# Order of the high and low products in a split-weight GEMM of a two-layer hybrid encoder

## The chip, the cores and the metric

The kernel runs on one core of a Trainium2 chip. The metric is the device time of one execution in microseconds (us): 2810.59 us is the median of three runs of the kernel before the change.

## What is computed

Two layers of a bidirectional encoder for one sequence of 256 tokens and 2048 channels, all in 32-bit floats:

```
u = RMSNorm(h);  z = u W_in                # 51 blocks of 128 columns
h += concat[A(z_A), B(z_B), C(z_C), D(z_D)] W_out
h += relu(RMSNorm(h) W_up)^2 W_down        # 2048 -> 8192 -> 2048
h += (p[i] W_ple) * sigmoid(RMSNorm(h) W_gate)
```

A is differential attention, B a gated linear recurrence (HGRN2), C a set of centred mean pools, D bidirectional RWKV-7 time mixing. Each works on 512 of the 2048 channels.

## The kernel before

Tokens are the free dimension (256 columns), channels lie on the partitions in chunks of 128. Every large product is a sum over chunks k of the contraction (16 for a contraction of 2048) of a 128x128 block of weights by a 128x256 piece of activations, into one PSUM tile of 128 output channels. Weights and activations are each kept as a high and a low part (of the type fp32r), and a product leaves out low by low.

**Weights.** `wsplit` (L132 to L144) loads 1024 weight columns (eight chunks k) with one DMA on SP, then for each 512 columns (a *part*, four chunks) ScalarE copies the high part `wh` (L140) and VectorE subtracts it from the raw weights for the low part `wl` (L142). `wh` and `wl` have two buffers each in the mixers and four in the pool `wide` behind them; the raw weights have four.

**Activations.** `split` stores each chunk as [hi | lo], 512 columns.

**Products.** For one chunk k, `mm2` (L154) issues two: `wh` by [hi | lo], 512 columns (L158), and then `wl` by hi, 256 columns (L159), which gives two half sums that `add_to` (L161) or its like adds later. `mm3` (L146) issues three of 256 columns (L150 to L152) into one half. Both products of a chunk come before those of the next chunk. `gemm_block` (L165) makes one block of 128 output channels: two loads of eight chunks each. It gets its PSUM tile from `K.accum`: pool `pg` with two buffers in the mixers and in the first half of the output projection, four (`pgw`) from then on.

**Stages of a layer.** The mixers call `z` (L225) for each block of `w_in`: 15 blocks for D with `mm3`, 36 for A, B and C with `mm2`. D works on four pairs of heads: `first` (L498), which needs neither an inverse nor the state, then `invert`, then `second` (L665) on the pairs 1, 3, 0, 2 with small products named psW, psX, psZ, pss, psst, psr, psy, psm and psv. Its result goes to DRAM through `put` (L414). What `first` leaves for `second` lies in a store `sp`; that of pair 0 is the tile `sp0`, which has the tag "h" and so the place of the residual h (L498). B's head makes its attention matrix in seven levels, each with a product psbl (L1015), a masked copy (L1017) and two multiplications (L1022, L1023) on VectorE and a rearranging copy (L1011) on ScalarE.

The output projection follows (L277 to L316), by `out_block`. Its contraction is cut in two: 12 chunks of mixer outputs that are done early (`mh1`, `w_out1`, with `mm2`) and 4 that are done last (`mh2`, `w_out2`, with `mm3`). Its h is loaded afresh from DRAM (L286 to L289) into the place with the tag "h". From block m = 9 on (L293) the weights come from the pool `wide`, which takes the room that the mixers held. The MLP (up and down in four quarters) and the gate with the per-layer embedding are `gemm_block` with `mm2`.

**Order.** The program text gives only the order in which the work is handed over. A scheduler then sets the order on each engine, by its own model of how long everything takes; so D's and B's small products stand among the products of `w_in` and of the output projection. DMAs are issued in the order in which they stand on SP.

Of the kernel before, what the change touches and what calls it, by code (L numbers as in the profile page):

```python
# [8 lines left out]
F32 = mybir.dt.float32  # L9
# [7 lines left out]
P = 128  # L17
# [35 lines left out]
# the output projection's contraction in the order in which the heads' outputs come  # L53
# [18 lines left out]
def trunk(ctx: ExitStack, tc: tile.TileContext, xT, pT, w_in, w_out1, w_out2, w_up, w_down, w_gate, w_ple, pvec,  # L72
# [10 lines left out]
    # every function used (Copy, Identity, Square, Exp, Ln) is in this one table set  # L83
    A.preload_act_table_set("natural_log_exp_and_others")

# [31 lines left out]
    # derived parameter columns  # L117
# [4 lines left out]
    # 0..14 token-shift own weight, 15..18 1-ka, 19 subln gain, 20..23 lb, 24..27 1-lb, 28 -lambda, 29..32 lb-1  # L122
# [9 lines left out]
    def wsplit(src, cols=1024):  # L132
        """Load weights and split them exactly into two float32r parts, in halves of 512 columns."""
# [12 lines left out]
    def mm3(ps, parts, b, act, start, stop):  # L146
        wh, wl = parts[b // 4]
        b %= 4
        w1, w2 = wh[:, b * P:(b + 1) * P], wl[:, b * P:(b + 1) * P]
        T.matmul(ps[:, :S], w1, act[:, :S], start=start, stop=False)  # L150
        T.matmul(ps[:, :S], w1, act[:, S:], start=False, stop=False)  # L151
        T.matmul(ps[:, :S], w2, act[:, :S], start=False, stop=stop)  # L152

    def mm2(ps, parts, b, act, start, stop):  # L154
        """The same with a weight part's loads shared: ps holds two halves, whose sum is the result."""
        wh, wl = parts[b // 4]
        b %= 4
        T.matmul(ps, wh[:, b * P:(b + 1) * P], act, start=start, stop=False)  # L158
        T.matmul(ps[:, :S], wl[:, b * P:(b + 1) * P], act[:, :S], start=False, stop=stop)  # L159
# [5 lines left out]
    def gemm_block(wsrc, m, act, mm=mm2, nk=KC, before=None):  # L165
        """One block of 128 output channels over nk chunks of the contraction."""
        ps = K.accum("acc")
        for u in range(nk // 8):
            w = wsplit(wsrc[m, u])
            for j in range(8):  # L170
                k = u * 8 + j
                if before is not None:
                    before(k)
                mm(ps, w, j, act[:, k], k == 0, k == nk - 1)
        return ps

    def split(dst, src, scale=None):
        """dst = [hi | lo] of src (times a per-channel scale)."""
# [7 lines left out]
    def rsqrt(dst, src, eps, scale=1.0):  # L186
        """dst = (src * scale + eps) ** -0.5"""
        A.activation(dst, src, AF.Ln, bias=eps, scale=scale)
        A.activation(dst, dst, AF.Exp, scale=-0.5)

    def sigmoid(dst, src, scale=None, bias=None):
        """dst = 1 / (1 + exp(-(src)))  ; bias is added to src (given already negated)."""
# [32 lines left out]
    def z(m, dst):  # L225
        """dst = a block of w_in's outputs. (D's, which come first, leave less of the vector engine's time.)"""
# [13 lines left out]
    def front():  # L240
        """Room for the next layer's input. It goes into w_in without RMSNorm's token scales, which come later."""
# [7 lines left out]
    def enter(c):  # L249
        """The first layer's input, a chunk of channels at a time."""  # L250
# [9 lines left out]
    for l in range(DEPTH):  # L260
# [7 lines left out]
        # in two parts: the second for the heads that are done last  # L268
# [8 lines left out]
        def out_block(wsrc, mh, n, mm):  # L277
            ps = K.accum("acc")
            for o in range(0, n, 8):
                nn = min(8, n - o)  # L280
                w = wsplit(wsrc[:, o * P:(o + nn) * P], nn * P)
                for j in range(nn):
                    k = o + j
                    mm(ps, w, j, mh[:, k], k == 0, k == n - 1)
# [7 lines left out]
        for m in range(KC):  # L292
            if m == 9:  # L293
                # outside the mixers there is room to load weights far ahead
# [19 lines left out]
        def norm():  # L314
            """The token scales of RMSNorm, applied to the products behind it."""
# [55 lines left out]
        for mm in range(4):  # L371
            pw = wsplit(w_ple[l, mm])
            for b in range(4):
                m = mm * 4 + b
                pp = pe.tile([P, 512], F32, tag="acc2", name="acc2", bufs=2)
                for k in range(2):
                    mm3(pp, pw, b * 2 + k, ph[:, k], k == 0, k == 1)
# [58 lines left out]
# w_in blocks in device order: D's wl, al, gl; D's k, r, v for the four pairs of heads; then four rounds of a C group,  # L436
# A's q, k, v (a head) and B's q, f, b, i, g (a head)
# What the first half of D's work on a pair of heads leaves to the second, in columns, for each direction.
# Instances are (head, chunk of 128 tokens); matrices are [s, t].
# [4 lines left out]
class MixerD:  # L444
    def __init__(self, K):
# [16 lines left out]
        # tanh(x) = 2 / (1 + exp(-2x)) - 1  # L462
# [27 lines left out]
    def slot(self, c):  # L490
        """A pair's place: the residual's or that of the MLP's input, which nothing else needs now."""
# [6 lines left out]
    def first(self, c, base):  # L498
        """All of a pair of heads that needs neither the inverse nor the state."""
# [10 lines left out]
        # normalised key direction  # L510
# [10 lines left out]
        # token-major v  # L521
# [12 lines left out]
        for d in range(2):  # L534
# [11 lines left out]
            # cumulative decay within chunks of 128, one pad column  # L546
# [23 lines left out]
            # [kk | r] with the decay up to t, [-b | k] with the inverse decay up to s  # L570
# [605 lines left out]
```

## Time and profile before

| what | value |
|---|---|
| median of 3 runs | 2810.59 us |
| lowest and highest run | 2810.06 and 2812.09 us |
| span of the profiled execution | 2811.6 us |
| instructions | 47293 |
| VectorE busy | 1986.4 us, 71% of the span |
| ScalarE busy | 1631.4 us, 58% |
| weights `wh` on ScalarE (L140) | 1704 times, mean 631 ns |
| weights `wl` on VectorE (L142) | 1704 times, mean 692 ns |
| bytes read from HBM | 471.51 MB |

No time was recorded for the profiled execution other than its span, which runs from the first recorded instruction to the last.

In the rows below PE is TensorE's multiplication, PEld its weight load (which overlaps PE), DVE VectorE, ACT ScalarE, SP the queue that issues DMAs. L158 is line 158 of the kernel. A duration of a matmul includes its passage through the array, so that two which follow each other overlap in the list: the distance between starts is the pace. The granted clock (PEclk) is a share of full speed.

### The profile page before, as it was taken

The numbers are of one execution on the slowest core, as the hardware profiler recorded it, in microseconds if no ns is written. First come the engines' busy times: TensorE is split into PE (matmuls) and PEld (weight loads), VectorE is DVE, ScalarE is ACT, GpSimd is POOL, SyncE is SP. The second block draws the span as 40 slices with busy tenths as digits, with TensorE's granted clock in tenths as the row PEclk, the third lists the DMA queues.
The fourth block names the chain that finished last, engine by engine and source line by source line (L and its number), as shares of the span: only waits on it lengthen the run. The fifth ranks groups of instructions, "written<-read, shape, count | busy, mean of one in ns | idle before, by whom it ended". The sixth has DMA issues, their size and how long they took to land.

```text
span 2811.6 us, 47293 instructions
## 1 busy us (share of the span) xinstructions
PE 2773.0 (99%) x16934; PEld 2378.5 (85%) x16934; DVE 1986.4 (71%) x4139; ACT 1631.4 (58%) x3342; POOL 57.5 (2%) x98
## 2 busy tenths in 40 slices
PE   8999999999999999999999999999999999999999
PEld 7877788898888888888898777888888888888888
DVE  7678877786666666667767697677766666666776
ACT  6555656476645546456765665565665465564565
POOL 0000110000000000000000001100000000000000
PEclk9999999999999999999999999999999999999999
DMA  6444445565555555555545444545655555555564
GB/s 211 151 138 142 157 125 194 198 198 187 187 187 187 187 185 185 186 187 197 173 161 161 128 150 148 167 145 177 199 187 188 187 187 184 188 185 187 187 198 158
DMA packets 186211, 494.40 MB, mean 176 GB/s; under 512 B 43732, under 2 KB 66900, under 8 KB 185848
## 3 DMA queue, kind: packets, MB, share of 16 engines
q1 hardware_dynamic: 185976, 491.39, 53.2%
q8 instruction: 133, 2.18, 0.3%
q14 instruction: 102, 0.84, 0.1%
HBM read 471.51 MB, written 19.80 MB: 175 GB/s over the span
## 4 chain that ended last, share of the span: by engine, by line
PE 92%; DVE 3%; ACT 2%; DMA 2%; issue 1%; POOL 0%; SPq 0%; DVEq 0%; POOLq 0%; ACTq 0%
PE acc L158 49%; PE acc L159 25%; PE acc L152 3%; PE acc L150 2%; PE acc L151 2%; PE psam L591 2%; DVE wl L142 1%; PE psbl L1015 1%; PE psrv L600 1%; PE pss L749 1%; PE psl L925 1%; ACT wh L140 1%; DMA raw<-in_w_out 1%; DMA ot<-o_scr 0%; PE psy L772 0%
## 5 line engine op out<-in xcount | busy, mean ns | idle before, releaser
L140 ACT ACTIVATE wh<-raw 128x512 fp32r<-128x512 f32 x1704 | 1073.7, 631 | 1023.1 <-PE acc L158 859.3
L142 DVE TENSOR_TENSOR wl<-raw,wh 128x512 fp32r<-128x512 f32 x1704 | 1177.1, 692 | 642.5 <-ACT wh L140 631.0
L158 PE MATMUL acc<-u,wh 128*128 128x512 f32 x3200 | 1154.0, 401 | 1.1 <-ACT wh L140 1.1
L159 PE MATMUL acc<-u,wl 128*128 128x256 f32 x3200 | 918.7, 288 | 7.8 <-DVE wl L142 7.4
L158 PEld LDWEIGHTS acc<-u,wh 128*128 128x128 f32 x3200 | 603.5, 189 | 146.2 <-ACT wh L140 5.7
L158 PE MATMUL acc<-act,wh 128*128 128x512 f32 x2048 | 723.9, 399 | 0.0
L159 PEld LDWEIGHTS acc<-u,wl 128*128 128x128 f32 x3200 | 606.1, 189 | 29.2 <-DVE wl L142 16.8
L159 PE MATMUL acc<-act,wl 128*128 128x256 f32 x2048 | 575.2, 281 | 0.0
L158 PEld LDWEIGHTS acc<-act,wh 128*128 128x128 f32 x2048 | 384.8, 188 | 96.2
L159 PEld LDWEIGHTS acc<-act,wl 128*128 128x128 f32 x2048 | 386.9, 189 | 0.0
L158 PE MATMUL acc<-ug,wh 128*128 128x512 f32 x512 | 181.6, 397 | 0.0
L150 PE MATMUL acc<-u,wh 128*128 128x256 f32 x480 | 137.9, 287 | 11.4 <-ACT u L183 9.8
L152 PE MATMUL acc<-u,wl 128*128 128x256 f32 x480 | 141.9, 296 | 2.2 <-DVE wl L142 2.0
L159 PE MATMUL acc<-ug,wl 128*128 128x256 f32 x512 | 143.4, 281 | 0.0
L158 PE MATMUL acc<-mh,wh 128*128 128x512 f32 x384 | 138.0, 398 | 0.7 <-ACT wh L140 0.6
L151 PE MATMUL acc<-u,wh 128*128 128x256 f32 x480 | 137.3, 286 | 0.7 <-DVE u L184 0.6
L158 PEld LDWEIGHTS acc<-ug,wh 128*128 128x128 f32 x512 | 96.0, 188 | 21.1
L159 PE MATMUL acc<-mh,wl 128*128 128x256 f32 x384 | 110.8, 289 | 0.9 <-DVE wl L142 0.9
L150 PEld LDWEIGHTS acc<-u,wh 128*128 128x128 f32 x480 | 91.8, 191 | 15.7 <-ACT u L183 10.0
L152 PEld LDWEIGHTS acc<-u,wl 128*128 128x128 f32 x480 | 91.6, 191 | 12.6 <-DVE wl L142 6.4
L159 PEld LDWEIGHTS acc<-ug,wl 128*128 128x128 f32 x512 | 96.7, 189 | 0.7
L151 PEld LDWEIGHTS acc<-u,wh 128*128 128x128 f32 x480 | 91.5, 191 | 2.5 <-DVE u L184 1.7
(320 smaller groups left out, 2808.4 us busy)
## 6 DMA issues: line engine op xcount, KB each, us to landing
raw<-in_w_up SPq DMA_DIRECT2D x256, 512.0 KB
raw<-in_w_down SPq DMA_DIRECT2D x256, 512.0 KB
raw<-in_w_in SPq DMA_DIRECT2D x204, 512.0 KB
raw<-in_w_gate SPq DMA_DIRECT2D x64, 512.0 KB
raw<-in_w_out SPq DMA_DIRECT2D x32, 512.0 KB
raw<-in_w_out SPq DMA_DIRECT2D x64, 256.0 KB
h<-in_xT SPq DMA_DIRECT2D x8, 512.0 KB
m_scr<-sp SPq DMA_DIRECT2D x16, 256.0 KB
```

The source lines that it names most:

```text
L140: A.activation(wh[:, :n], raw[:, o:o + n], AF.Copy)
L142: V.tensor_tensor(wl[:, :n], raw[:, o:o + n], wh[:, :n].bitcast(F32), ALU.subtract)
L150: T.matmul(ps[:, :S], w1, act[:, :S], start=start, stop=False)
L151: T.matmul(ps[:, :S], w1, act[:, S:], start=False, stop=False)
L152: T.matmul(ps[:, :S], w2, act[:, :S], start=False, stop=stop)
L158: T.matmul(ps, wh[:, b * P:(b + 1) * P], act, start=start, stop=False)
L159: T.matmul(ps[:, :S], wl[:, b * P:(b + 1) * P], act[:, :S], start=False, stop=stop)
L591: T.matmul(ps[:, x * S:(x + 1) * S], BK[hs, j, x, :], KR[j][hs].rearrange("p a b -> p (a b)"), start=True, stop=True)
L600: T.matmul(pv_[hs, S + j * P:S + (j + 1) * P], vt[:, j, hs], AV[:, 1, :], start=False, stop=True, skip_group_check=True)
L749: T.matmul(ps[:, d * P + h * 64:d * P + (h + 1) * 64], Zs[d][:, h * 2 + j, :], rk(d, j)[:, h] if st == 0 else RH[:, d, h, :], start=True, ...
L925: T.matmul(pl[:, :S], qn[ms, qs], kn[ms, :], start=True, stop=True)
L1015: T.matmul(p2[:, i * P:(i + 1) * P], kc[:, i * P:(i + 1) * P], strided(Q, i * P, [[2 * hh, P // (2 * hh)], [W + hh, 2], [1, hh]]), start=T ...
```

## The change

`mm2` and `mm3` no longer take one chunk but one part of the weights and a group of its chunks, four of them (two for `w_ple`): all products with the high part come first, then all with the low part. The callers pass groups: `gemm_block`, `out_block` and the product with `w_ple`. `before(k)`, with which a caller splits an input chunk just ahead of its product, is called for the four chunks of a group ahead of the group. No instruction is added or removed; the sums are added up in another order. (In the changed kernel these functions stand a few lines further down: L161 and L163 are what L158 and L159 were.)

```diff
-    def mm3(ps, parts, b, act, start, stop):
-        wh, wl = parts[b // 4]
-        b %= 4
-        w1, w2 = wh[:, b * P:(b + 1) * P], wl[:, b * P:(b + 1) * P]
-        T.matmul(ps[:, :S], w1, act[:, :S], start=start, stop=False)
-        T.matmul(ps[:, :S], w1, act[:, S:], start=False, stop=False)
-        T.matmul(ps[:, :S], w2, act[:, :S], start=False, stop=stop)
...
+    def mm3(ps, part, group):
+        wh, wl = part
+        for b, act, start, stop in group:
+            w1 = wh[:, b * P:(b + 1) * P]
+            T.matmul(ps[:, :S], w1, act[:, :S], start=start, stop=False)
+            T.matmul(ps[:, :S], w1, act[:, S:], start=False, stop=False)
+        for b, act, start, stop in group:
+            T.matmul(ps[:, :S], wl[:, b * P:(b + 1) * P], act[:, :S], start=False, stop=stop)
...
-        T.matmul(ps, wh[:, b * P:(b + 1) * P], act, start=start, stop=False)
-        T.matmul(ps[:, :S], wl[:, b * P:(b + 1) * P], act[:, :S], start=False, stop=stop)
+        for b, act, start, stop in group:
+            T.matmul(ps, wh[:, b * P:(b + 1) * P], act, start=start, stop=False)
+        for b, act, start, stop in group:
+            T.matmul(ps[:, :S], wl[:, b * P:(b + 1) * P], act[:, :S], start=False, stop=stop)
...
-            for j in range(8):
-                k = u * 8 + j
+            for o in range(0, 8, 4):
+                ks = range(u * 8 + o, u * 8 + o + 4)
                 if before is not None:
-                    before(k)
-                mm(ps, w, j, act[:, k], k == 0, k == nk - 1)
+                    for k in ks:
+                        before(k)
+                mm(ps, w[o // 4], [(k % 4, act[:, k], k == 0, k == nk - 1) for k in ks])
...
-                for j in range(nn):
-                    k = o + j
-                    mm(ps, w, j, mh[:, k], k == 0, k == n - 1)
+                for i in range(0, nn, 4):
+                    ks = range(o + i, o + i + 4)
+                    mm(ps, w[i // 4], [(k % 4, mh[:, k], k == 0, k == n - 1) for k in ks])
```

Since the scheduler works out its order anew, the small products move too. Three places follow. All are of TensorE in the first layer's output projection; `acc<-mh` are the products of a block (`wh` the high, `wl` the low part), the others belong to the mixers, and a final number as in x4 counts equal rows.

First, the second block of the projection. Before the change:

```order
L158 MATMUL acc<-mh_5837,wh 128x512
L719 MATMUL psX<-U_2734,sp_1115 64x64 x4
L1015 MATMUL psbl<-bQ,bkc 128x128 x2
L159 MATMUL acc<-mh_5837,wl 128x256
L158 MATMUL acc<-mh_5837,wh 128x512
L159 MATMUL acc<-mh_5837,wl 128x256
```

With the change:

```order
L161 MATMUL acc<-mh_5837,wh 128x512 x4
L951 MATMUL psan<-t_5425,cst 128x256
L992 MATMUL psbv<-cst,z 128x128 x2
L163 MATMUL acc<-mh_5837,wl 128x256 x4
L161 MATMUL acc<-mh_5837,wh 128x512 x4
L723 MATMUL psX<-U_2571,sp_2565 64x64 x4
L163 MATMUL acc<-mh_5837,wl 128x256 x4
```

Where high and low products took turns, four high ones now precede four low ones, and small products stand between the two fours.

Second, the stretch behind the second block. Before the change small products stand singly among those of the blocks:

```order
L159 MATMUL acc<-mh_5837,wl 128x256
L1015 MATMUL psbl<-bQ,bkc 128x128 x2
L158 MATMUL acc<-mh_5837,wh 128x512
L749 MATMUL pss<-sp_1115,Tm 128x64 x2
L159 MATMUL acc<-mh_5837,wl 128x256
```

With the change, from the last product of the second block on (66 small products stand before the third block; the first of them):

```order
L163 MATMUL acc<-mh_5837,wl 128x256 x4
L1006 MATMUL psbd<-x_5434,bkc 128x128 x2
L1019 MATMUL psbl<-bQ,bkc 128x128 x2
L729 MATMUL psZ<-Tm,W 64x64 x4
L753 MATMUL pss<-sp_2565,Tm 128x64 x2
L1019 MATMUL psbl<-bQ,bkc 128x128 x2
L753 MATMUL pss<-sp_2565,Tm 128x64 x2
L1019 MATMUL psbl<-bQ,bkc 128x128 x2
L760 MATMUL psst<-SA,sp_2565 64x64 x4
L1019 MATMUL psbl<-bQ,bkc 128x128 x2
L744 MATMUL psr<-S_2673,sp_2565 128x128 x2
L1019 MATMUL psbl<-bQ,bkc 128x128 x2
```

The third block's products have moved behind all of these; `sp_2565` is the store of pair 0, in the place of h.

Third, the end of D's last `second`, ahead of block m = 9. Before the change:

```order
L159 MATMUL acc<-mh_5837,wl 128x256
L785 MATMUL psm<-t_2878,cst 128x256
L158 MATMUL acc<-mh_5837,wh 128x512
...
L790 MATMUL psv<-t_2884,cst 128x256
L159 MATMUL acc<-mh_5837,wl 128x256
```

With the change; the last row but one is the first of block m = 9:

```order
L163 MATMUL acc<-mh_5837,wl 128x256 x4
L776 MATMUL psy<-sp_1115,SA 64x128 x2
L781 MATMUL psy<-sp_1115,S_2836 128x128
L776 MATMUL psy<-sp_1115,SA 64x128 x2
L781 MATMUL psy<-sp_1115,S_2836 128x128
L789 MATMUL psm<-t_2878,cst 128x256
L794 MATMUL psv<-t_2884,cst 128x256
L161 MATMUL acc<-mh_5837,wh 128x512 x4
L163 MATMUL acc<-mh_5837,wl 128x256 x4
```

The products of a block that stood between psy, psm and psv now stand ahead of all three.

## Rows read from the trace of the kernel before

**Rows 1.** The page: busy time and the chain that ended last, shares of the span.

```profile
PE 2773.0 (99%) x16934; PEld 2378.5 (85%) x16934; DVE 1986.4 (71%) x4139; ACT 1631.4 (58%) x3342; POOL 57.5 (2%) x98
...
PE 92%; DVE 3%; ACT 2%; DMA 2%; issue 1%; POOL 0%; SPq 0%; DVEq 0%; POOLq 0%; ACTq 0%
```

**Rows 2.** L158 in a stretch of the MLP: us; PE, PEld busy (count); PEclk; DMA share; GB/s.

```profile
800.00:900.00 100.00, 100.00 (x284) 53.18 (x283) 1.00 0.56 188
```

**Rows 3.** Who waited until a weight part was made: all low parts; L158 (us, times).

```profile
  DVE wl L142: 35.9, 70
...
  ACT wh L140: 8.9, 22
```

**Rows 4.** Timeline in the mixers: start, us, engine, line, operation [idle before <- releaser].

```profile
250.83 0.42 DVE L1023 TENSOR_TENSOR bK<-bK,bF 128x256 f32<-128x256 f32 x1
...
251.00 0.39 PE L158 MATMUL acc<-u,wh 128*128 128x512 f32 x1
...
251.50 0.68 DVE L142 TENSOR_TENSOR wl<-raw,wh 128x512 fp32r<-128x512 f32 x1
...
252.24 0.39 PE L159 MATMUL acc<-u,wl 128*128 128x256 f32 x1 [0.85 <-DVE wl L142]
```

**Rows 5.** Groups by line and form: count | busy us, mean ns | idle before.

```profile
L159 PE MATMUL acc<-u,wl 128*128 128x256 f32 x3200 | 918.7, 288 | 7.8 <-DVE wl L142 7.4
...
L159 PE MATMUL acc<-act,wl 128*128 128x256 f32 x2048 | 575.2, 281 | 0.0
...
L152 PE MATMUL acc<-u,wl 128*128 128x256 f32 x480 | 141.9, 296 | 2.2 <-DVE wl L142 2.0
```

**Rows 6.** Windows (PE, PEld, DVE, ACT, POOL; PEclk; DMA; GB/s) and a timeline row.

```profile
348.00:351.00 3.00, 1.34 (x20) 1.07 (x20) 1.44 (x4) 2.00 (x7) 0.53 (x1) 1.00 1.02 419
351.00:355.00 4.00, 4.00 (x20) 3.49 (x19) 2.54 (x5) 1.59 (x4) 0.00 (x0) 0.52 0.59 168
...
1740.40:1747.20 6.80, 6.80 (x29) 6.01 (x27) 4.08 (x8) 2.31 (x6) 0.00 (x0) 0.50 0.52 158
...
350.79 0.38 PE L725 MATMUL psZ<-Tm,W 64*64 64x64 f32 x3 [1.28 <-ACT W L722]
```

**Rows 7.** Timeline of TensorE in the MLP.

```profile
589.68 0.62 PE L158 MATMUL acc<-u,wh 128*128 128x512 f32 x2
590.13 0.28 PE L159 MATMUL acc<-u,wl 128*128 128x256 f32 x1
590.25 0.40 PE L158 MATMUL acc<-u,wh 128*128 128x512 f32 x1
590.49 0.28 PE L159 MATMUL acc<-u,wl 128*128 128x256 f32 x1
```

**Rows 8.** Timeline rows ahead of block m = 9.

```profile
516.50 0.44 PE L772 MATMUL psy<-sp,SA 128*64 128x128 f32 x4
...
522.81 0.59 PE L790 MATMUL psv<-t,cst 128*128 128x256 f32 x2
...
526.42 0.42 DVE L796 TENSOR_TENSOR t<-t,bg 128x256 f32<-128x256 f32 x1
...
528.04 1.85 SPq L135 DMA_DIRECT2D raw<-in_w_out  x4
...
532.62 1.67 ACT L140 ACTIVATE wh<-raw 128x512 fp32r<-128x512 f32 x3 [0.36 <-DMA raw<-in_w_out]
```

**Rows 9.** Tile h from 460 to 500 us: ns min/median/max, first and last start us.

```profile
L289 SPq DMA_DIRECT2D h<-in_xT x4: 327/424/430, 471.5 to 472.8; - x4
L162 DVE TENSOR_TENSOR h<-h,acc x2: 420/421/422, 485.9 to 493.9; 128x256 f32<-128x256 f32 x2
```

**Rows 10.** Timeline of TensorE, two levels of a B head.

```profile
247.31 0.60 PE L1015 MATMUL psbl<-bQ,bkc 128*128 128x128 f32 x4
...
249.38 0.61 PE L1015 MATMUL psbl<-bQ,bkc 128*128 128x128 f32 x4
...
249.74 0.36 PE L159 MATMUL acc<-u,wl 128*128 128x256 f32 x1
```

More of the change, by code (lines that the diff above doesn't have):

```diff
@@ L144, in wsplit, with mm2 @@
         return parts
-    def mm3(ps, parts, b, act, start, stop):
-        wh, wl = parts[b // 4]
-        b %= 4
-        w1, w2 = wh[:, b * P:(b + 1) * P], wl[:, b * P:(b + 1) * P]
-        T.matmul(ps[:, :S], w1, act[:, :S], start=start, stop=False)
-        T.matmul(ps[:, :S], w1, act[:, S:], start=False, stop=False)
-        T.matmul(ps[:, :S], w2, act[:, :S], start=False, stop=stop)
-    def mm2(ps, parts, b, act, start, stop):
-        wh, wl = parts[b // 4]
-        b %= 4
-        T.matmul(ps, wh[:, b * P:(b + 1) * P], act, start=start, stop=False)
-        T.matmul(ps[:, :S], wl[:, b * P:(b + 1) * P], act[:, :S], start=False, stop=stop)
+    def mm3(ps, part, group):
[6 more added lines that the diff above has]
+            T.matmul(ps[:, :S], wl[:, b * P:(b + 1) * P], act[:, :S], start=False, stop=stop)
+    def mm2(ps, part, group):
+        wh, wl = part
+        for b, act, start, stop in group:
+            T.matmul(ps, wh[:, b * P:(b + 1) * P], act, start=start, stop=False)
+        for b, act, start, stop in group:
+            T.matmul(ps[:, :S], wl[:, b * P:(b + 1) * P], act[:, :S], start=False, stop=stop)
     def add_to(dst, ps):
@@ L375, in trunk @@
                 pp = pe.tile([P, 512], F32, tag="acc2", name="acc2", bufs=2)
-                for k in range(2):
-                    mm3(pp, pw, b * 2 + k, ph[:, k], k == 0, k == 1)
+                mm3(pp, pw[b // 2], [((b * 2 + k) % 4, ph[:, k], k == 0, k == 1) for k in range(2)])
                 ps = ahead.pop(0) if ahead else gemm_block(w_gate[l], m, u)
```

## The prediction

> **What bounds the kernel now.** I read the page's busy times and slices first, then the groups by line, then who waits for the weights, then the stretches where TensorE thins out. [rows 1] TensorE is busy for 99% of the span and 92% of the chain that ended last is its own work, so only what changes on TensorE, or what leaves it without work, moves the end. [rows 2] In the MLP it never waits: 283 loads of a high part in 100 us, a pair of products (512 columns with the high part, called W here, then 256 with the low part, called w) every 0.353 us. That holds for the 4608 pairs of up, down and gate (by the loops 2048 + 2048 + 512). What is lost lies in the mixers, where VectorE and ScalarE also run the heads.
>
> Three losses show there. [rows 3] First, weights that come late: TensorE and its weight loads sat idle 35.9 us, 70 times, until VectorE had made a low part, and 8.9 us until ScalarE had made a high one. [rows 4] One of them: W starts at 251.00, VectorE makes bK first and starts the low part only at 251.50, and w starts at 252.24, 1.24 us after W instead of the 0.24 of rows 7; the product then takes 0.39 us instead of 0.28, since the weight load behind it could not go ahead. [rows 5] That lengthening is a mean of 288 ns against the MLP's 281 over 3200 products and 296 over 480: 22 + 7 us. So late low parts cost 36 + 29 = 65 us, late high parts 9. Second, chains of small products with nothing between them. [rows 6] From 348 to 351 us TensorE is busy 1.34 of 3 us; psZ waits 1.28 us for ScalarE. Third, the clock behind it: [rows 6] the granted clock is 1.00 (2.4 GHz) in that stretch and 0.52 (1.2 GHz but for its start) in the next. The second layer has the same at 1740.4 us, and there it stays at 0.50 for 6.8 us, some 3.4 us of work lost.
>
> **The change, part by part.** It adds and removes no instruction. It puts four W, then four w.
>
> *Late low parts.* A w is due three W later, 3 x 0.23 = 0.7 us, and high buffers come free earlier. That would cover all but the longest waits, whose mean is 35.9 / 70 = 0.5 us. But the order of the change shows that the scheduler now puts the small products between the four W and the four w, and these wait for VectorE operations that stand ahead of the next low part in its queue. So much of the grace is spent at once. Bounds: nothing, and all of 65 + 9 = 74 us. I take 28, about four tenths of the low parts' waits: of the 408 low groups of w_in more than a quarter, 117, have such small products right ahead of them, and others have them among the four W before.
>
> *Pace.* The same columns are streamed and the same 128-column loads made. [rows 7] Two W in a row stand at 589.68; the next product starts at 590.13, so 0.225 us each; w follow at 0.12. Bounds: 0.225 + 0.117 = 0.342 for a pair gives 4608 x -0.011 = -51 us; 0.24 + 0.12 gives +31. Between these I take 2 ns less for a pair, -8 us, close to nothing, because the pair behind that place takes 0.36, and the gain of 0.02 us there (0.45 + 0.12 for two W and a w, against 2 x 0.236 + 0.117) may be one of phase alone. The Trainium skill, "TensorE: Matmul & The Clock Gate", section "Back-to-back issue gap", gives columns / 2.4 + 2.5 ns at full clock, whatever the order: an estimate of 325 ns for a pair. The trace differs, with 353 ns; by that rule this term is 0 and the sum 8 us more.
>
> *Block 9 of the output projection.* This is the first new stop. Its weights go into a pool that takes the mixers' room, and SP issues them only behind the last result of D. [rows 8] Before: psy from 516.50, psv at 522.81, the result ready at 526.42 + 0.42, the weights' DMA at 528.04, the high part made from 532.62; all of that beside the products of the blocks before, and ScalarE waits 0.36 us for the DMA. In the change psy, psm and psv stand directly ahead of block 9, with no product beside them. The chain then: psy four groups of 0.44, VectorE 0.4, psm 0.6 like psv, VectorE and ScalarE 0.4 each, psv to the result 3.6 (4.03 before, less one 0.4 of other work in between), the result's DMA issued in 0.5 (a quarter of 1.85), 4.6 from the weights' DMA to ScalarE's start, the high part 0.6: 12.9 us, of which about 2 is TensorE's own work. 11 us in each layer, 21 for both after half a microsecond each that is lost today. Bounds 7 and 16 each, by how much of the 4.6 us landing is queueing.
>
> *Third block of the output projection.* It needs one of two accumulators, and so block 0's addition into h, and so h's load. h takes the place of a head pair's store, which psy reads last. [rows 9] Before, that load is issued from 471.5 us on and the first addition runs at 485.9, just when block 0 is done: no wait. In the change D's second part on that pair comes later: 66 small products stand between the second and third block of the first layer, 57 in the second. The B chain in it went at one psbl in 2.07 us [rows 10] (of that VectorE alone needs three operations like the 0.42 of bK, 1.3 us): psbd 0.6, five steps 10.4, the last psbl 0.6, psy 1.8, then the load 0.5 + 4.6 as in rows 8 and two additions 0.8: 19.3 us. Their own work is 132 passes (two for each float32 product); four passes of 128 columns take 0.36 us (from 249.38 to 249.74) [rows 10], and most here are narrower, so about 9 us. So 10 to 11 us, and 9 to 10 in the second layer, with fewer products: 20 together. Bounds 12 and 30.
>
> *Other runs.* In the second layer two more of them stand with 13 and 10 waiting products, in some ten steps; each can lose what psZ lost, 1.28 us, and I take a third of it: 4 us. The two runs of today are taken apart: twice the 3 - 1.34 of rows 6, -3. Sum +1, bounds -3 and +10.
>
> *Clock.* The four stops at blocks 2 and 9 leave TensorE without half its work for longer than the stretch of rows 6 did. If each is followed by the same 6.8 us at 1.2 GHz, 4 x 3.4 = 13.6 us, less the two of today, 6.8: +7. Bounds 0 and 17. The Trainium skill, "TensorE: Matmul & The Clock Gate", section "Part 1: The HAM clock gate", says the same: a TensorE that idles is set back to half rate; the trace agrees, 0.52 and 0.50 behind the idle stretch.
>
> *DMA and the other queues.* Weight loads follow the freeing of buffers; a high part's comes free up to 0.35 us earlier. DMA engines are busy for 0.56 of the time [rows 2], so this is hidden.
>
> Sum: -28 - 8 + 21 + 20 + 1 + 7 = +13 on the profiled 2811.6 us; that execution stands 1.0 us above the median of the runs, so 2811.6 + 13 - 1.0 = **2824 us**, slower by 0.5%.
>
> **Rivals.** (a) *The late weights go entirely* (faster). Place: the low groups in the mixers; price: 74 instead of 28 us, so 2824 - 46 = 2778. It decides from about 47 of the 74 us on. For it: the grace of 0.7 us exceeds the mean wait; the example's 1 us is a long one. Against it: the small products ahead of the low groups. Chance 0.22. (b) *Alternating itself costs* (faster). If a row of W runs at 0.225 throughout, -51 instead of -8: 2781. For it: the one row; against: the slower pair behind it. Chance 0.06. (c) *The stops are half as long* because the load of h or of block 9's weights lands sooner and the chains run at VectorE's 1.3 us a step: 42 us of stops and clock become 28 or so, and the result lies within measurement at about 2811. Chance 0.16. (d) That the change does not do what it says is excluded: its order shows fours everywhere in the MLP.
>
> **How the numbers follow.** A difference of 0.2%, 5.6 us, is about what a measurement of this kernel can tell from none. Forecast, slower than 2816: 0.56. Within 0.2%: 0.16, rival (c). Faster: 0.22 + 0.06 = 0.28. The forecast's own range, with its terms' inner bounds, is 2810 to 2858. The range of 8 in 10 reaches down into (a) and (b), whose lower halves are left out: 2785 to 2860.
>
> **What would show it.** Right: in the changed profile TensorE has two gaps in each layer near 490 and 530 us (1880 and 1920), of about 10 us each, ended by the addition into h and by block 9's high part; the granted clock is near 0.5 behind each; idle before low parts falls from 36 us to 15 to 25; the MLP still takes 100 us for 282 to 286 pairs. Wrong: no such gaps or gaps under 5 us; idle before low parts under 5 us; 290 or more pairs in 100 us, which is rival (b); or fewer than 278, which would make it far slower.

## The result and the profile after

| kernel | median us | runs | lowest to highest |
|---|---|---|---|
| before | 2810.32 | 4 | 2810.01 to 2812.09 |
| with the change | 2832.18 | 4 | 2830.42 to 2833.38 |

The change makes the kernel slower: ratio 1.0074, 95% interval 1.006 to 1.0088, or 21.9 us. The profiled execution took 2832.92 us; its span is 2831.2 us.

The page of the changed kernel, the lines that answer to [rows 1] (busy time, then the chain that ended last):

```profile
PE 2762.6 (98%) x16934; PEld 2375.6 (84%) x16934; DVE 1971.8 (70%) x4139; ACT 1633.1 (58%) x3342; POOL 55.8 (2%) x98
...
PE 94%; DVE 3%; ACT 1%; DMA 1%; issue 0%; SPq 0%; DVEq 0%; ACTq 0%
```

The same products take less busy time in a longer span: TensorE stands still more. Who waited until a low part was made (all low parts, us and times), which answers to [rows 3], and the groups of low products that answer to [rows 5] (count | busy us, mean ns | idle before):

```profile
  DVE wl L142: 10.1, 22
...
L163 PE MATMUL acc<-u,wl 128*128 128x256 f32 x3200 | 521.8, 285 | 2.3 <-DVE wl L142 2.2
L163 PE MATMUL acc<-act,wl 128*128 128x256 f32 x2048 | 325.8, 281 | 0.0
...
L155 PE MATMUL acc<-u,wl 128*128 128x256 f32 x480 | 79.7, 287 | 0.0
```

So most late weights did go: 10.1 us of idle time instead of 35.9, and the low products lengthen by 4 and 6 ns on the MLP's 281 instead of 7 and 15. (Busy sums of grouped products leave out their overlap; only means compare.)

These sums of idle time are not time lost, though. The 35.9 us add the idle time of TensorE and that of its weight loads. The waits for low parts of the kernel before, of TensorE and then of its weight loads (us, times, longest), and the weight load that belongs to the late product of [rows 4]:

```profile
PE acc L159 <- DVE wl L142: 8.4, 16, 1.7
PE acc L152 <- DVE wl L142: 2.0, 6, 0.7
...
PEld acc L159 <- DVE wl L142: 19.1, 35, 2.0
...
PEld acc L152 <- DVE wl L142: 6.4, 13, 0.9
...
252.24 0.19 PEld L159 LDWEIGHTS acc<-u,wl 128*128 128x128 f32 x1 [1.17 <-DVE wl L142]
```

48 weight loads waited, and TensorE stood with 22 of them; those waits are counted twice (1.17 and 0.85 us for a product that came 1.00 us late). By the distances between starts, taken as for the table below, these 48 products and the ones right behind them began about 22 us late in all. After the change 17 were late, by about 5.5 us.

TensorE in a stretch of the MLP, high products alone, beside [rows 2] (us; PE busy (count); PEld busy (count); PEclk; DMA share; GB/s):

```profile
800.00:900.00 100.00, 77.89 (x287) 48.82 (x286) 1.00 0.57 187
```

Counted from the starts, 285 pairs begin in these 100 us against 283: 350.8 ns for a pair instead of 353.3. From the first product of the MLP to the last of the gate it takes 3.8 us less in the first layer and 3.9 in the second.

The time is lost at the two places that the order showed. First, ahead of the third block; the timeline of TensorE from the last product of the second block to the first of the third (start, us, engine, line, operation [idle before <- releaser]):

```profile
471.44 0.74 PE L163 MATMUL acc<-mh,wl 128*128 128x256 f32 x4
472.02 0.61 PE L1006 MATMUL psbd<-x,bkc 128*128 128x128 f32 x4
472.46 0.82 PE L1019 MATMUL psbl<-bQ,bkc 128*128 128x128 f32 x4
...
477.29 0.68 PE L1019 MATMUL psbl<-bQ,bkc 128*128 128x128 f32 x4 [0.30 <-DVE bQ L1026]
...
483.47 0.49 PE L781 MATMUL psy<-sp,S 128*128 128x128 f32 x2
483.79 0.61 PE L1019 MATMUL psbl<-bQ,bkc 128*128 128x128 f32 x4
...
489.54 1.20 PE L161 MATMUL acc<-mh,wh 128*128 128x512 f32 x4 [0.61 <-DVE h L167]
```

No single wait is long (0.61 us at most here, 1.21 in the second layer). From product to product it is 17.63 us (16.03 in the second layer) with 132 and 112 passes of small products in them. The B head takes seven levels from 472.46 to 483.79, 1.9 us each; psy ends at 484, and the tile view of h then shows the load and the first addition, beside [rows 9]:

```profile
L166 DVE TENSOR_TENSOR h<-h,acc x5: 415/422/422, 488.1 to 506.3; 128x256 f32<-128x256 f32 x5
...
L294 SPq DMA_DIRECT2D h<-in_xT x4: 328/427/433, 484.0 to 485.3; - x4
```

Second, block 9, beside [rows 8]; the timeline of all engines:

```profile
530.31 0.49 PE L781 MATMUL psy<-sp,S 128*128 128x128 f32 x2
...
531.31 0.70 PE L789 MATMUL psm<-t,cst 128*128 128x256 f32 x2 [0.51 <-DVE t L787]
...
532.97 0.70 PE L794 MATMUL psv<-t,cst 128*128 128x256 f32 x2 [0.96 <-ACT t L792]
...
536.67 0.33 SPq L419 DMA_DIRECT2D o_scr<-t  x1
537.04 1.87 SPq L135 DMA_DIRECT2D raw<-in_w_out  x4
...
541.11 1.67 ACT L140 ACTIVATE wh<-raw 128x512 fp32r<-128x512 f32 x3 [5.38 <-DMA raw<-in_w_out]
...
541.79 1.65 PE L161 MATMUL acc<-mh,wh 128*128 128x512 f32 x3 [8.12 <-ACT wh L140]
```

TensorE is still from psv to 541.79. The chain is the one that the prediction wrote down: result, its DMA at 536.67, the weights' DMA at 537.04, ScalarE at 541.11. From block 8 to block 9 it is 12.85 us, in the second layer 12.79. And the clock behind it (windows; PE, PEld, DVE, ACT, POOL; PEclk; DMA; GB/s), beside [rows 6], with the stretch at 326, the first products of the third block, and the end of D's blocks of w_in in both layers:

```profile
326.00:334.00 8.00, 5.96 (x40) 5.27 (x39) 7.28 (x17) 2.54 (x6) 2.71 (x3) 1.00 0.81 280
...
492.00:496.00 4.00, 4.00 (x29) 3.26 (x28) 2.45 (x6) 2.46 (x6) 0.00 (x0) 1.00 0.32 98
533.00:542.00 9.00, 0.88 (x3) 0.48 (x4) 1.50 (x4) 2.38 (x5) 0.00 (x0) 0.65 0.46 140
542.00:549.00 7.00, 7.00 (x29) 5.91 (x30) 5.54 (x11) 4.15 (x9) 0.00 (x0) 0.71 1.04 331
...
129.60:143.20 13.60, 11.55 (x34) 8.29 (x34) 7.60 (x22) 2.45 (x5) 0.00 (x0) 0.50 0.07 27
1535.90:1546.10 10.20, 7.10 (x19) 5.43 (x20) 7.68 (x23) 4.39 (x10) 0.00 (x0) 0.50 0.15 53
```

The granted clock falls to 1.2 GHz in and behind the stop at block 9 (0.65 and 0.71 as means), and also at a place that the order did not show: from 129.6 to 143.2 us and from 1535.9 to 1546.1 it is 0.50, in and behind a wait of psam (below). Behind the third block it stays at 2.4 GHz in this profile, and the slow stretches of before at 351 and 1740 us are gone. In all, and without the last few us of the execution, the changed kernel spends 47.8 us at 1.2 GHz and the kernel before 17.1; the mean granted clock is 0.991 instead of 0.996. The Trainium skill, "TensorE: Matmul & The Clock Gate", section "Part 1: The HAM clock gate", has an idle TensorE set back to half rate; this trace agrees at block 9 and at psam.

Last, what is new in the waits of TensorE (us in total, times, longest):

```profile
PE acc L161 <- ACT wh L140: 16.2, 2, 8.1
PE psam L595 <- DVE BK L583: 8.8, 2, 4.4
...
PE psbl L1019 <- DVE bQ L1026: 4.0, 6, 2.0
```

The first is block 9. The others are the heads' own chains: psam at the end of D's blocks waits 4.4 us in each layer with nothing beside it, where before its waits for VectorE came to 0.6 us in all. The lower clock of the last two windows begins in this wait and goes on behind it.

A sum over the trace puts this together. For each kind of product I took the unstalled distance from its start to the next one (the mean of those within 25 ns of the fastest tenth, in the kernel before) and called what a distance exceeds it by *lost*:

| stretch | lost before, layers 1 and 2 | lost after, layers 1 and 2 | difference |
|---|---|---|---|
| D's 15 blocks of w_in, up to the next block | 31.5, 25.1 | 32.6, 26.2 | +2.2 |
| other 36 blocks of w_in | 69.0, 67.1 | 56.6, 63.2 | -16.3 |
| projection, up to block 2 | 1.9, 2.1 | 9.8, 9.9 | +15.7 |
| projection, blocks 2 to 8 and the way to 9 | 5.2, 6.3 | 15.7, 16.4 | +20.6 |
| blocks 9 to 15 | 0.8, 0.9 | 2.3, 1.7 | +2.3 |
| the rest of the layer | 1.8, 1.9 | -2.0, -2.0 | -7.7 |

Together +16.8; the small products, more of which now follow each other, are 3.5 us dearer in their unstalled distances. That is 20.3 us, against the 19.7 by which the last product starts later (2824.5 against 2804.8).

### The profile page after: what moved, and what is told of

Read it like the earlier page. It is cut to its first block, busy times and chain, and to the rows that moved or that the text cites. A ratio compares the mean times of both kernels' runs of the same rounds, so it can differ in the third digit from the quotient of the medians.

```text
span 2831.2 us, 47352 instructions
## 1 busy us (share of the span) xinstructions
PE 2762.6 (98%) x16934; PEld 2375.6 (84%) x16934; DVE 1971.8 (70%) x4139; ACT 1633.1 (58%) x3342; POOL 55.8 (2%) x98
## 4 chain that ended last, share of the span: by engine, by line
PE 94%; DVE 3%; ACT 1%; DMA 1%; issue 0%; SPq 0%; DVEq 0%; ACTq 0%
PE acc L161 50%; PE acc L163 26%; PE acc L155 3%; PE acc L152 3%; PE acc L153 3%; PE psam L595 2%; PE psrv L604 1%; PE psbl L1019 1%; DVE wl L142 1%; PE psl L929 1%; PE pss L753 0%; PE psy L776 0%; PE psrv L601 0%; DMA h<-in_xT 0%; PE psw L544 0%
## 5 line engine op out<-in xcount | busy, mean ns | idle before, releaser
L161 PE MATMUL acc<-u,wh 128*128 128x512 f32 x3200 | 885.6, 398 | 3.6 <-DVE z L237 3.4
L161 PEld LDWEIGHTS acc<-u,wh 128*128 128x128 f32 x3200 | 549.2, 189 | 88.2 <-DVE z L237 4.4
L161 PE MATMUL acc<-act,wh 128*128 128x512 f32 x2048 | 559.0, 394 | 0.0
L163 PEld LDWEIGHTS acc<-u,wl 128*128 128x128 f32 x3200 | 484.7, 189 | 75.3 <-DVE wl L142 6.4
L163 PE MATMUL acc<-u,wl 128*128 128x256 f32 x3200 | 521.8, 285 | 2.3 <-DVE wl L142 2.2
L161 PEld LDWEIGHTS acc<-act,wh 128*128 128x128 f32 x2048 | 350.0, 189 | 47.0
L163 PEld LDWEIGHTS acc<-act,wl 128*128 128x128 f32 x2048 | 314.3, 189 | 43.6
L163 PE MATMUL acc<-act,wl 128*128 128x256 f32 x2048 | 325.8, 281 | 0.0
L161 PE MATMUL acc<-ug,wh 128*128 128x512 f32 x512 | 139.4, 395 | 0.0
L161 PE MATMUL acc<-mh,wh 128*128 128x512 f32 x384 | 108.9, 406 | 18.0 <-ACT wh L140 16.2
L166 DVE TENSOR_TENSOR h<-h,acc 128x256 f32<-128x256 f32 x160 | 67.2, 421 | 83.0 <-PE acc L163 78.9
L152 PEld LDWEIGHTS acc<-u,wh 128*128 128x128 f32 x480 | 91.9, 192 | 14.7 <-ACT u L188 8.8
L161 PEld LDWEIGHTS acc<-ug,wh 128*128 128x128 f32 x512 | 88.0, 189 | 12.0
L153 PEld LDWEIGHTS acc<-u,wh 128*128 128x128 f32 x480 | 91.7, 191 | 4.1 <-issue 2.0
L161 PEld LDWEIGHTS acc<-mh,wh 128*128 128x128 f32 x384 | 67.0, 193 | 28.5 <-ACT wh L140 17.0
L163 PEld LDWEIGHTS acc<-ug,wl 128*128 128x128 f32 x512 | 77.9, 189 | 10.2
L163 PE MATMUL acc<-ug,wl 128*128 128x256 f32 x512 | 81.1, 281 | 0.0
L155 PE MATMUL acc<-u,wl 128*128 128x256 f32 x480 | 79.7, 287 | 0.0
```

Source lines behind the costliest of these rows:

```text
L166: V.tensor_tensor(dst, dst, ps[:, S:], ALU.add)
```

## The experiments

All are built on the changed kernel with a group size `g` for each caller; `g = 1` is the order of before:

```diff
-    def mm2(ps, part, group):
+    def mm2(ps, part, group, g=GM):
...
-        for b, act, start, stop in group:
-            T.matmul(ps, wh[:, b * P:(b + 1) * P], act, start=start, stop=False)
-        for b, act, start, stop in group:
-            T.matmul(ps[:, :S], wl[:, b * P:(b + 1) * P], act[:, :S], start=False, stop=stop)
+        for s in range(0, len(group), g):
+            for b, act, start, stop in group[s:s + g]:
+                T.matmul(ps, wh[:, b * P:(b + 1) * P], act, start=start, stop=False)
+            for b, act, start, stop in group[s:s + g]:
+                T.matmul(ps[:, :S], wl[:, b * P:(b + 1) * P], act[:, :S], start=False, stop=stop)
```

`mm3` likewise. Where D's blocks take turns, `before(k)` stands just ahead of its product again. GD is the group in D's blocks of w_in, GZ in the others, GO in the projection, GM in MLP, gate and w_ple. In these kernels L163 is the high and L165 the low product. Each edit lets the scheduler work out the whole order anew, so a run shows an edit together with all that moved with it. Medians of before in the three sets of runs were 2810.32, 2810.05 and 2809.75 us.

### Which part costs

**e1: MLP and gate alone.**

```diff
+GZ, GD, GO, GM = 1, 1, 1, 4
```

> Groups of four only in up, down, gate and w_ple; w_in and the output projection take turns as before, so the order in the mixers is that of the kernel before. Theory (the MLP gains 2.2 ns for each of its 4608 pairs, since 100 us of the changed kernel's MLP come 0.7 us earlier than before's): 10 us faster than before, 2800. Rival (that drift belongs to what the mixers leave behind, such as late loads, and not to the order of the products): no change, 2810.

Measured 2807.09 us, ratio 0.9994 (0.9981 to 1.0007). The drift is there: its profile gains 3.8 and 3.9 us from MLP to gate, as the changed kernel's. But part of the 10 us is given back. TensorE's timeline ahead of the MLP's norm:

```profile
594.75 0.63 PE L165 MATMUL acc<-u,wl 128*128 128x256 f32 x4
596.75 0.70 PE L218 MATMUL ssq<-ssacc,onesd 128*128 128x256 f32 x2 [1.37 <-DVE ssacc L215]
```

The norm's product waits 1.37 us in each layer. In the second layer's first block of w_in one product, whose high part is late, starts 2.8 us behind its neighbour instead of 1.0, and 3.4 us at the lower clock follow; that layer's mixers and projection take 3.9 us longer than before. The theory held for the pace, not for the whole time.

**e2: w_in alone.**

```diff
+GZ, GD, GO, GM = 4, 4, 1, 1
```

> Groups of four only in w_in. Its order keeps the run of small products ahead of the third block of the output projection (54 and 56 of them) and lets D's last products stand among those of blocks 4 to 8. Theory (the third-block stop comes from the grouping in w_in, the block-9 stop from both together): the third-block stop stays at some 15 us from product to product in each layer, the one at block 9 goes, time 2812 to 2822. Rival (both stops come from the grouping in the projection itself): no stop in either place and only the gain of the late weights, 2770 to 2795.

Measured 2832.80 us, ratio 1.0084 (1.0056 to 1.0112). The third-block stop stays (18.2 and 15.2 us), as the theory had it; but block 9 stops too, 8.9 and 7.7 us, without any group in the projection. Both theories were wrong on block 9. The clock, too, is not as in the changed kernel: in the run of small products ahead of the third block it falls to 1.2 GHz, although TensorE is busy in it and was busy 4.83 of the 6 us before (view as in [rows 6]):

```profile
480.30:490.50 10.20, 10.10 (x44) 7.58 (x44) 5.49 (x16) 1.25 (x3) 0.31 (x1) 0.50 0.11 36
```

**e3: the projection alone.**

```diff
+GZ, GD, GO, GM = 1, 1, 4, 1
```

> Groups of four only in the output projection. Theory (stops come from w_in): no gap over 3 us between blocks, within 4 us of before, 2806 to 2812. Rival (the projection's own grouping makes the stops): 20 us or more slower, 2830 and above.

Measured 2826.62 us, ratio 1.0057 (1.0041 to 1.0073). No third-block stop, but 9.4 and 8.3 us at block 9. Neither theory had that: a stop at block 9 although products of blocks 7 and 8 stand beside D's last ones. The timeline shows a step of it (TensorE, ScalarE, VectorE and SP):

```profile
526.72 0.59 PE L793 MATMUL psm<-t,cst 128*128 128x256 f32 x2
526.96 1.27 PE L163 MATMUL acc<-mh,wh 128*128 128x512 f32 x4
...
527.73 0.41 DVE L794 TENSOR_TENSOR t<-t,psm 128x256 f32<-128x256 f32 x1
528.07 0.63 PE L165 MATMUL acc<-mh,wl 128*128 128x256 f32 x4
528.27 0.63 ACT L141 ACTIVATE wh<-raw 128x512 fp32r<-128x512 f32 x1 [1.19 <-PE acc L163]
528.54 1.09 PE L163 MATMUL acc<-mh,wh 128*128 128x512 f32 x4
528.81 0.40 ACT L796 ACTIVATE t<-t 128x256 f32<-128x256 f32 x1
...
529.47 0.64 PE L165 MATMUL acc<-mh,wl 128*128 128x256 f32 x4
...
529.95 0.59 PE L798 MATMUL psv<-t,cst 128*128 128x256 f32 x2
...
533.54 0.33 SPq L423 DMA_DIRECT2D o_scr<-t  x1
533.93 1.86 SPq L136 DMA_DIRECT2D raw<-in_w_out  x4
```

D's next step on ScalarE (L796) could run at 528.1, when VectorE is done, but stands behind a high part that waits 1.19 us for its buffer, which four high products hold; and psv stands behind two whole groups. From psm to psv it is 3.23 us, before the change 2.05. In the order of TensorE, D's and B's small products stand mostly 7 to 9 products apart in the kernel before (around the first high product of a part) and mostly 12 or 16 apart here (between groups). So D's last result comes at 533.5 instead of 526.9 us (57.7 us behind the projection's first product instead of 47.1), and block 9, whose weights wait for it, at 539.2.

**e7 and e8: D's blocks alone, and those of A, B and C alone.**

```diff
+GZ, GD, GO, GM = 1, 4, 1, 1
...
+GZ, GD, GO, GM = 4, 1, 1, 1
```

> Groups of four only in the 15 blocks of w_in that D reads. Theory (in the changed kernel D's stage came out even: 6.4 us ahead after its first slice, 0.7 after the second, with a new stall of 4.7 us): 2806 to 2816. Rival (D's stage is where most of the 22 us are lost): 2820 or more.

> Groups of four only in the 36 blocks of w_in that A, B and C read. 49 and 56 small products stand ahead of the third block of the projection. Theory (this part alone makes the third-block stops, and by late heads those at block 9 too): gaps of 14 to 18 us ahead of block 2 and of 6 to 9 ahead of block 9, 2824 to 2836. Rival (it needs the groups in D's blocks too): 2805 to 2815.

e7: 2823.32 us, ratio 1.0044 (1.0029 to 1.0059), above the theory's 2816 and in the rival's range: besides the stall of 4.7 us at psam (from start to start), which is there in both layers, block 9 of the second layer stops for 4.75 us. e8: 2825.10 us, ratio 1.0056 (1.004 to 1.0073), a time that the theory had, with 12.6 and 15.2 us ahead of block 2, 9.3 and 7.1 us ahead of block 9. (The profile is that of its fastest run, 2809.41 us; why that one is faster is told at the end.) So each of the three parts alone (D's blocks, the others of w_in, the projection) costs 13 to 16 us, and together they cost less than their sum. Why is not shown. That all three delay the same chain is not the whole of it: in e7's first layer D's last result comes at 520.6 us, earlier than before, and block 9 does not stop.

### Whether block 9's stop is the late last result

**e4: the changed kernel, the pool opened three blocks later.**

```diff
-            if m == 9:
+            if m == 12:
```

> The changed kernel with the pool for far-ahead weights opened at block 12 instead of block 9, so that three more blocks can stand beside D's last products; the third-block run of 66 and 65 small products stays. Theory (in the changed kernel block 9 stands 12.85 us behind block 8, some 1.7 of it work, and its products take 2 us longer at the lower clock): 13 us less in each layer, 2832 - 26 = 2806, slightly faster than before. Rival (the stop only moves to block 12): 2828 to 2834.

Measured 2826.53 us, ratio 1.0065 (1.004 to 1.009): below the rival's range, but nearer to it than to the theory. The stop moved to block 12, 8.6 and 5.0 us. D's last result came 7 us later than in the changed kernel, at 543.6 us instead of 536.7, since the order had put its steps among the three more blocks. That left two readings: the late result, or the opening itself.

**e5: e3 with the pool at block 15; e6: groups in the projection only from block 9 on and in its second part; e9: the changed kernel with the pool at block 15.**

```diff
+GZ, GD, GO, GM = 1, 1, 4, 1
...
-            if m == 9:
+            if m == 15:
```

```diff
+GZ, GD, GO, GM = 1, 1, 1, 1
...
-        def out_block(wsrc, mh, n, mm):
+        def out_block(wsrc, mh, n, mm, g=4):
...
-            ps = out_block(w_out1[l, m], mh1, NOUT1, mm2)
+            ps = out_block(w_out1[l, m], mh1, NOUT1, mm2, 4 if m >= 9 else 1)
```

> As the run with groups in the output projection alone, with the pool for far-ahead weights opened at block 15 instead of 9. Theory now (D's last result comes late, at 533.5 instead of 526.9 us, because the groups set the steps of its chain 16 products apart instead of 8; block 9 follows it 5 to 6 us later): six more blocks stand beside that, both gaps of 9.4 and 8.3 us go, 2806 to 2813. Rival (opening the pool costs 8 us wherever it stands, as block 12 had 8.6 and 5.0): 2822 to 2830.

> Groups of four in the output projection only from block 9 on and in its second part; blocks 0 to 8 take turns, so D's chain stands as in the kernel before. Theory (the loss comes from the groups in blocks 0 to 8, beside D's chain): no gap over 2 us, 2806 to 2812. Rival (groups cost in the projection itself, by late weights): 2820 or more.

> The changed kernel with the pool for far-ahead weights opened at block 15. Theory (the pool waits for D's late last result, as the run with groups in the projection alone showed): the gaps of 8.6 and 5.0 us that still stood at block 12, and 2 us at the lower clock behind each, go; 2826.5 - 17.6 = 2809, range 2804 to 2813. The gaps ahead of the third block stay (66 and 65 small products). Rival (the pool's opening costs wherever it stands here): 2822 or more.

e5: 2796.70 us, ratio 0.9969 (0.9948 to 0.999). No gap over 1.7 us is left between blocks, and where the second layer's MLP begins, after the same amount of products, it is 17.5 us ahead of e3: the two stops and what their clock cost. (The total lies below the expectation for a reason of the MLP's pace, told at the end.) e6: 2809.78 us, ratio 0.9999 (0.999 to 1.0009): groups cost nothing where no head's chain runs beside them. e9: 2811.15 us, ratio 1.0008 (0.9995 to 1.0022), 21.0 us less than the changed kernel; between blocks 11 and 15 no gap over 0.7 us is left, though D's last result still comes at 543.6. So the opening is free; what costs is a late last result with nothing left to multiply. This alone undoes nearly the whole loss.

### Whether both stops can be had away

**e10: e9 with D's pairs in another order.**

```diff
-    for c in (1, 3, 0, 2):
+    for c in (3, 0, 1, 2):
...
-MIX = [8, 0, 4, 9, 1, 5, 10, 15, 2, 13, 6, 11, 14, 3, 12, 7]
+MIX = [8, 0, 4, 9, 1, 5, 10, 15, 2, 12, 6, 11, 14, 3, 13, 7]
```

> As the run before it, and D's pairs are finished in the order 3, 0, 1, 2 instead of 1, 3, 0, 2 (the projection's contraction takes pair 0 where it took pair 1), so that h's place comes free earlier; no small products stand alone ahead of the third block now, but in the first layer D's last products stand directly ahead of block 15. Theory (the third-block stops cost some 9 us in each layer; one stop of some 11 us remains at block 15): 2809 - 18 + 11 = 2802, range 2795 to 2808. Rival (the small products cost the same wherever they stand): 2806 to 2816 with the stop.

Measured 2825.13 us, ratio 1.0055 (1.0036 to 1.0073): outside both ranges, 14 us slower than e9. The third-block stop is gone (1.9 and 1.3 us), but D's last result is at 558.9 us, and block 15 stops in both layers, 13.1 and 10.2 us, where the order had shown it for the first only. The timeline of the first layer:

```profile
553.01 0.70 PE L791 MATMUL psm<-t,cst 128*128 128x256 f32 x2 [0.51 <-DVE t L789]
554.67 1.22 PE L796 MATMUL psv<-t,cst 128*128 128x256 f32 x2 [0.96 <-ACT t L794]
563.76 1.65 PE L163 MATMUL acc<-mh,wh 128*128 128x512 f32 x3 [7.87 <-ACT wh L141]
```

By the sum of the table above, e10 loses some 16 us less than e9 up to block 2 and some 30 more in blocks 9 to 15. That the heads get on in a third-block stop, so that the time comes back at the end of D's chain when it is taken away, is a reading of this: the new order of the pairs may itself have made that chain end later.

**e11: what the runs spoke for; e12: its two moves without any group.**

```diff
+GZ, GD, GO, GM = 4, 1, 1, 4
...
-AHEAD = 2
+AHEAD = 3
```

```diff
+GZ, GD, GO, GM = 1, 1, 1, 1
```

Both have the pool at block 15 and the pairs of e10; in e11 gate and w_ple take turns.

> Groups of four in the w_in blocks of A, B and C and in up and down; turns in D's blocks, the output projection, the gate and w_ple; pool at block 15, pairs in the order 3, 0, 1, 2, and three instead of two blocks ahead of the norm. Its order has no run of small products in the projection. Theory (without the stops the late weights saved remain, some 24 us in both layers by the run with A, B and C alone, and 8 of the MLP): 2778, range 2772 to 2790. Rival (the time saved in w_in is only small products put off): 2798 or more.

> The kernel before, all in turns, with the pool at block 15 and the pairs in the order 3, 0, 1, 2. Theory (in turns there was no stop to remove): 2806 to 2811. Rival (these two moves gain by themselves): 2800 or less.

e11: 2796.07 us, ratio 0.9955 (0.9938 to 0.9972), faster than both kernels, but less than half of the way to the forecast: where the MLP begins, after the same amount of products, its profile stands 7.8 us ahead of before in the first layer, and the second layer's mixers and projection add 2.8, not 24 in all. Most of what w_in saves was small products put off, as the rival said: from D's last block to the projection it takes 20.2 and 17.7 us less than before, and from there to the MLP 13.8 and 14.2 us more. e12: 2784.16 us, ratio 0.9915 (0.9895 to 0.9935), the fastest of all and against the theory. Yet the moves gained next to nothing themselves (1.7 us where the first MLP begins, 0.6 in the second layer's mixers and projection); 27 us came in the two MLPs and gates, which nothing in this kernel touches. High products in the MLP, at the same places as in [rows 2], in e12:

```profile
800.00:900.00 100.00, 100.00 (x290) 53.91 (x289) 1.00 0.59 191
2300.00:2400.00 100.00, 100.00 (x289) 53.94 (x289) 1.00 0.58 189
```

288 pairs begin in 100 us instead of 283: 346.7 ns for a pair, in both layers, in the same order of products.

## Why the prediction was right, and where it was off

The forecast was 2824 us, slower, by four stops that outweigh the late weights; measured were 2832.2. The two places, the two layers and the sign came as written. Of what was to show it, three things did not come: ahead of the third block TensorE does not stand in a gap but works through 132 passes of small products, the clock behind it stays at 2.4 GHz, and idle time before low parts fell to 10.1 us, below the 15 to 25 of the text. Its steps in turn:

- **Late low parts.** This term was mis-sized most. The text prices them at 36 + 29 = 65 us and takes 28 off. But the 36 count a wait twice where TensorE and its weight load both stood, and of the 29 us of lengthening about 5 belong to products that had waited at all. By the distances between starts the price was about 22 us, and 16.5 of them went: three quarters, not the four tenths of the text. That the two errors partly cancel is luck. The mixers as a whole lost only 14 us less (+2.2 and -16.3 in the table), where the sum has 28. Beside the saving, these rows hold psam's new waits of 8.8 us and the lower clock behind them, for which the sum had no term in D's stage, and the two slow stretches that went. This is +14 on the forecast, and the largest error.
- **Pace.** 2 ns less for a pair was taken, 2.5 measured; the MLP and gate gain 7.7 us net of the norm's wait. The formula in the Trainium skill, "TensorE: Matmul & The Clock Gate", section "Back-to-back issue gap", which that section gives for an isolated product, made an estimate of 325 ns for a pair; the trace has 350.8 in groups and 353.3 or 346.7 in turns, and the measurement decides.
- **Block 9.** 12.9 us from block to block were worked out, 12.85 and 12.79 measured; the table's row with the way to block 9 lost 20.6 us more, for 21 in the sum. That the weights' DMA waits for D's last result is confirmed by e9: given six more blocks beside it, the stops go and 21.0 us with them.
- **Third block.** 19.3 us were worked out, 17.63 and 16.03 measured; lost were 15.7 in both layers, against 20. Whether they are a cost by themselves stays open: e9 keeps both of these stops and takes as long as the kernel before, and e10, without them, is slower than e9 by other stops.
- **Clock.** Four stretches of 3.4 us, less two, were taken as +7. Behind block 9 the lower clock came: from its first product to its last it took 6.1 and 5.6 us instead of 3.9, and blocks 9 to 15 lost 2.3 us more in all. Behind the third block it did not, and the two stretches of before went. It came behind psam instead, 13.7 and 10.2 us long, where the prediction had no stop.
- **Other runs.** Small, as taken; but the small products' own time grew by 3.5 us, which was not in the sum.

So 13 became 20: +14 for the mixers, -5 for the clock behind the stops, -4 for the third block, -1 for the other runs, which stand in the mixers' rows, and +3.5 for the small products. The reason given, that small products now stand in a row, was true and not the root: e3 and e6 show that groups beside a head's chain make the last head end later (57.7 us behind the projection's first product, against 47.1 with turns), and the kernel pays where the products that could cover it run out. How much of this is the wider spacing on TensorE and how much ScalarE's queue is not taken apart. Rival (a) had a wrong price, since all late low parts together were worth 22 us and not 65; rival (b) fell with the pace, rival (c) with the measured chains (its 42 us for stops and clock leave the clock's 7 out).

## What to carry to other kernels

Where small dependent products run beside large ones on one engine, ask of a new order not only what it saves the large ones, but how many of them now stand between two steps of the small chain, and where that chain's last result is waited for. Look for the place where the cover runs out, and give it more work beside it: that brought back 21.0 of 21.9 us, with all groups of four left in place. And reorder only where no chain runs beside: there it cost nothing (e6), or gained less than the runs can tell from none (e1). Count a wait once: idle time of an engine and of its weight loads can be the same wait, and the distance between starts says what it cost.

## What was not expected of the hardware

The same alternating products run at two paces. In the kernel before 353.3 ns for a pair is the rule; but 346.7 ns stands in the whole MLP of the first layer in the profiles of e2 (289 loads of a high part in 800 to 900 us, 283 in 2300 to 2400) and e8, of the second layer in that of e5, and of both in e12. Each such MLP is worth some 13.5 us, and times come in steps to match: the 50 runs of before lie mostly at 2807 to 2814 us, with six at 2794 to 2802; seven of nine of e5 at 2796 to 2799; one of five of e8 at 2809, the others at 2824 to 2829; all four of e12 at 2784 to 2787. In groups only 350.8 ns was seen (the ten runs of e1 lie within 5 us). The pace keeps from the start of an MLP to its end. Three rows of TensorE's timeline in e12:

```profile
800.33 0.39 PE L163 MATMUL acc<-act,wh 128*128 128x512 f32 x1
800.56 0.28 PE L165 MATMUL acc<-act,wl 128*128 128x256 f32 x1
800.68 0.39 PE L163 MATMUL acc<-act,wh 128*128 128x512 f32 x1
```

Here a high product takes 230 ns to the next start where before it took mostly 233, 236 and 241; the low one takes 116.7 ns on average in both. But in the fast MLPs of e2 and e5 the means are 231.7 and 115.0 ns, so it is the pair that is 6.6 ns shorter each time, and not always by the same product. What decides the pace was not tried and stays open; so does whether e12 would keep its time in other surroundings.
